# Weight splits moved into the norms, roots by a GpSimd power, and three smaller moves in a two-block transformer kernel

## The chip, the cores and the metric

One core of one Trainium2 chip. The metric is the device time of one execution in microseconds (us); the median of several executions is compared. Weights and activations are in fp32, in DRAM at the start; the output goes back to DRAM. Five engines take part, each with its own queue of instructions that it runs in order: TensorE (PE: matmul; PEld: its weight loads), VectorE (DVE), ScalarE (ACT), GpSimd (POOL) and SyncE (SP, which only issues DMAs here).

## The reference

256 tokens of width 1024 go through two blocks. The first mixes (block attention beside a gated linear recurrence, hgrn2), then has a product-key expert layer (PEER). The second has two layers with adaptive modulation: an even one (convolution beside an RG-LRU) and an odd one (stick-breaking attention), each with a SwiGLU feed-forward.

```python
def rmsnorm(x, g):
    y = x * lax.rsqrt(jnp.mean(x * x, axis=-1, keepdims=True) + 1e-6)
    return y * g

# first block
xn = rmsnorm(h, norm1_g)
q_a, k_a, v_a, q_r, f_r, i_r, g_r = split(xn @ w_in)
h = h + concat([moba_attention(q_a, k_a, v_a), hgrn2(q_r, f_r, i_r, g_r, lb, rec_norm_g)]) @ w_out
h = h + peer(rmsnorm(h, norm2_g), wq, subkeys, peer_u, peer_v)
x = rmsnorm(h, normf_g)

# hgrn2: f = lb + (1-lb)*sigmoid(f_pre), per head and chunk
scores = einsum('bhtd,bhtsd,bhsd->bhts', qc, exp(min(cum_t - cum_s, 0)), kc)   # decay products
o = rmsnorm(o, norm_g) * silu(g)

# peer: top 16 of 128 x 128 keys per head
gates = softmax(sc)                       # sc: the 16 best scores
out = einsum(gates * gelu(xb @ u[eidx]), v[eidx])

# second block, each layer
sh_m, sc_m, g_m, sh_f, sc_f, g_f = split(silu(c) @ ada_w + ada_b)
x = x + g_m * mixer(rms_norm(x, mix_norm) * (1 + sc_m) + sh_m)
hf = rms_norm(x, ffn_norm) * (1 + sc_f) + sh_f
x = x + g_f * ((silu(hf @ w_gate) * (hf @ w_up)) @ w_down)
# odd mixer: q = rms_norm(qkv[0], q_norm), k = rms_norm(qkv[1], k_norm), per head of 64
```

## The kernel before

All products are in fp32 precision, made of three matmuls of split operands: every weight half (128x1024, 512 KB, one DMA on SP into `raw`, L180) is split into `hi`, a cast on ScalarE (L197), and `lo = raw - hi`, on VectorE (L198), on GpSimd for six units of wq and six of pu. Two halves are a unit. The weights form one stream in a fixed order: wp (input projection), wo, wq (queries), pu and pv (experts), wi0, wo0, fgu0, fd0, wi1, wo1, fgu1, fd1. `unit` (L203) hands out a unit and loads the next one; at the last three units of wo, pv and fd it loads two ahead, so that two units of the next stream are there when that stream's norm runs. There are four `raw` buffers, and three (in places eight) of `hi` and `lo`.

In front of wp, wq, wi0, fgu0, wi1 and fgu1 stands a norm, `norm_t` (L403). For each half of the tokens `t` (128 tokens) it adds the residual (`add_res`: L778, or L781 and L782 with a gate row), squares on ScalarE with a sum (L480), adds the sums up into `m` (L428; L434 to L436 where a second gain row comes in), takes its root with `rsqrt1` (L379: a guess by integer arithmetic and three Newton steps, eight VectorE operations), scales an identity by it (`dr`, L440), turns the tokens on TensorE by 16 matmuls with `dr` (L448), and makes `y` (ScalarE, L451) and its split `xh` and `xl` (L458, L459). After the first half of the tokens, `ahead` (L328) multiplies it with the first two units, whose `hi` and `lo` must be there; the second half is normed beside that and multiplied in `out_n512` (L308), whose result is then copied out by ScalarE (L345), and the following unit's splits are queued behind that copy (`evict`, L226).

In mix1 the recurrence makes the decay products chunk by chunk: differences (L609, L611), their exponentials (ScalarE, L612), then the product with the keys on GpSimd (L613) and with the queries on VectorE (L614); L641 does the cross part. At the end each half of the tokens goes through a root of 128x4 (`rsqrt`, L365: ten VectorE operations), the gate product `o` (L759, L760), transposes, and the copy `ch` (L765), the operand of wo. Attention logits are `lg` (L661).

In peer the routing runs as a generator, one step per expert, beside the expert matmuls. `gains` (L869) is the softmax of the gates: a difference `gr` on VectorE (L872), two steps, an Exp for each token half on ScalarE (L876), a step, and the normalising (L880 to L882). ScalarE's other work there is the experts' activation `actA` (L990), of another function table, so that each change of function costs a table load (ACT_TABLE_LOAD). In the odd layer `qk` (L1316) takes roots of 128x8 (L1326) for queries and keys.

The adaptive modulation (`ada_steps`, L1081) is a second background: 96 products of 128x1024 on VectorE (L1118), each with its own 512 KB DMA `araw`, taken one step at a time by the loops of the other stages, in the even layer by `chunk` (L1215).

The order of work on each engine is made by a list scheduler, which takes the program's order as priority; `issue_after(ins)` says that what follows is queued behind `ins` on that engine. `self.after` holds the last two operations of a norm, behind which later splits are queued.

Of the kernel before, what the change touches and what calls it, by code (L numbers as in the profile page):

```python
# [137 lines left out]
class Prog:  # L138
# [4 lines left out]
    def stream_init(self):  # L143
# [10 lines left out]
        self.pending = []  # L154
        self.nload = 0
# [18 lines left out]
    def load(self, n, hs=(0, 1)):  # L174
        nc = self.nc
        nm, j = self.order[n]
        halves = self.ready.setdefault(n, [])
        for h in hs:
            s = self.wp.tile([128, 1024], F32, name="raw", bufs=self.RAWB)
            self.last_load = nc.sync.dma_start(s, self.i[nm][j][:, h * 1024:(h + 1) * 1024])  # L180
            pool, bufs = self.wp, self.SPB
            if self.roomy(n):
                if self.ring % (self.SPB + self.EXT) >= self.SPB:
                    pool, bufs = self.ext, self.EXT
                self.ring += 1
            else:
                self.ring = 0
            hi = pool.tile([128, 1024], F32R, name="hi", bufs=bufs)
            lo = pool.tile([128, 1024], F32R, name="lo", bufs=bufs)
            a, b = self.POOLED.get(nm, (0, 0))  # L190
            eng = nc.gpsimd if a <= j < b else nc.vector
            with ExitStack() as es:
                for i in self.after:
                    es.enter_context(self.tc.issue_after(i))
                if self.evicted is not None:
                    es.enter_context(self.tc.issue_after(self.evicted.ins))
                nc.scalar.copy(hi, s)  # L197
                ins = eng.tensor_tensor(lo, s, hi.bitcast(F32), op=ALU.subtract)  # L198
            if eng is nc.vector:
                self.last_lo = ins  # L200
            halves.append((hi, lo))

    def unit(self, nm, j):  # L203
# [8 lines left out]
        if self.nload <= upto:  # L212
            self.load(self.nload, (0,))
            self.half = self.fresh = True
        return self.ready.pop(n)

    half = fresh = False

    def rest(self):

        if self.half:
            self.half = False
            self.load(self.nload, (1,))
            self.nload += 1
# [136 lines left out]
    def guess(self, y, x):  # L361

        self.nc.vector.tensor_scalar(y.bitcast(I32), x.bitcast(I32), -0.5, float(0x5f3759df), op0=ALU.mult, op1=ALU.add)

    def rsqrt(self, pool, v, n, scale):  # L365

        nc = self.nc
        x = pool.tile([128, n], F32, name="rx", bufs=2)
        y = pool.tile([128, n], F32, name="ry", bufs=2)
        z = pool.tile([128, n], F32, name="rz", bufs=2)  # L370
        nc.vector.tensor_scalar(x, v, scale, EPS, op0=ALU.mult, op1=ALU.add)
        self.guess(y, x)
        for _ in range(3):
            nc.vector.tensor_tensor(z, y, y, op=ALU.mult)
            nc.vector.scalar_tensor_tensor(z, z, -0.5, x, op0=ALU.mult, op1=ALU.mult)
            nc.vector.scalar_tensor_tensor(y, z, 1.5, y, op0=ALU.add, op1=ALU.mult)
        return y

    def rsqrt1(self, pool, x):  # L379

        nc = self.nc
        m = pool.tile([128, 1], F32, name="rm", bufs=4)
        y = pool.tile([128, 1], F32, name="r1", bufs=4)
        z = pool.tile([128, 1], F32, name="r2", bufs=4)
        self.guess(y, x)
# [794 lines left out]
    def even(self):  # L1180
# [34 lines left out]
        def chunk(n):  # L1215
# [3 lines left out]
            if n % 2:  # L1219
                next(st, None)  # L1220
# [227 lines left out]
```

## Time and profile before

| what | us |
|---|---|
| median of 3 runs | 1647.27 (1646.49 to 1650.29) |
| the profiled execution | 1649.3 |
| its span in the profile | 1647.5 |
| TensorE busy | 1591.6 |
| VectorE busy | 1253.1 |
| ScalarE busy | 868.9 |
| GpSimd busy | 80.3 |

The mean granted TensorE clock over the span was 0.992 of full speed. Three views were read: the page's first part for the share of each engine; the list of what TensorE waited for, one line for each pair of waiting and releasing line; and the timeline around the waits, in which a figure in brackets after an instruction is the engine's idle time before it, with what ended it. A stretch's granted clock comes from the table of stretches; 1.00 is the upper level (2.4 GHz), 0.50 the lower (1.2 GHz), and a value between is a mean over both.

### The profile page before, as it was taken

What the parts mean: (1) busy time and instruction counts of PE and PEld (TensorE: products, weight loads), DVE (VectorE), ACT (ScalarE), POOL (GpSimd) and SP (SyncE); (2) the same over time, 40 slices, a digit from 0 to 9 for tenths busy, and PEclk for the clock granted to TensorE, in tenths of its full rate; (3) what the DMA queues carried; (4) which work ended last, traced back from release to release, by engine and by line L of the source; (5) the groups of instructions that cost most, each with busy time, mean ns of one, the idle gap of its engine ahead of it and who ended that gap; (6) DMA issues with size and microseconds to landing.
All of it is one profiled execution on the core that took longest, in us unless ns stands there. A gap on an engine that the chain in (4) does not pass through costs nothing.

```text
span 1647.5 us, 25992 instructions
## 1 busy us (share of the span) xinstructions
PE 1591.6 (97%) x9406; PEld 1394.1 (85%) x9406; DVE 1253.1 (76%) x2840; ACT 868.9 (53%) x1581; POOL 80.3 (5%) x47
## 2 busy tenths in 40 slices
PE   7999998999999999999999998999999999999998
PEld 6877898999999999888887886887888877778887
DVE  5987489958888898777778777886888778656553
ACT  5654554545444444455555555745444477755441
POOL 0120481000000000000000000000000000000000
PEclk9999999999999999999999999999999999999999
DMA  6435354644444444877778876565999653327552
GB/s 205 141 104 168 104 179 143 207 139 151 146 152 150 146 151 152 283 264 262 271 272 271 270 270 206 179 229 186 336 333 333 244 195 119 102 94 242 185 186 72
DMA packets 89041, 323.00 MB, mean 196 GB/s; under 512 B 9904, under 2 KB 10320, under 8 KB 88784
## 3 DMA queue, kind: packets, MB, share of 16 engines
q1 hardware_dynamic: 87904, 317.88, 56.7%
q10 hardware_dynamic: 1008, 3.47, 0.6%
q8 instruction: 73, 1.20, 0.3%
q14 instruction: 56, 0.46, 0.1%
HBM read 320.24 MB, written 1.06 MB: 195 GB/s over the span
## 4 chain that ended last, share of the span: by engine, by line
PE 82%; DVE 8%; ACT 5%; DMA 4%; issue 2%; ACTq 0%; DVEq 0%; SPq 0%
PE acc L277 16%; PE acc L279 16%; PE acc L278 16%; PE pt L249 8%; PE pt L250 8%; PE pt L253 8%; PE acc L976 3%; DVE lo L198 2%; ACT hi L197 2%; DMA raw<-in_wi 1%; PE pt L448 1%; DMA raw<-in_wo 1%; ACT y L451 1%; PE pt L620 1%; ACT jk L480 1%
## 5 line engine op out<-in xcount | busy, mean ns | idle before, releaser
L198 DVE TENSOR_TENSOR lo<-raw,hi 128x1024 fp32r<-128x1024 f32 x476 | 580.7, 1224 | 245.3 <-ACT hi L197 236.9
L197 ACT CAST hi<-raw 128x1024 fp32r<-128x1024 f32 x500 | 523.3, 1051 | 385.5 <-PE acc L279 144.3
L249 PE MATMUL pt<-xh,hi 128*128 128x256 f32 x1344 | 336.9, 288 | 11.7 <-ACT actA L990 6.8
L250 PE MATMUL pt<-xl,hi 128*128 128x256 f32 x1344 | 330.8, 284 | 0.0
L249 PEld LDWEIGHTS pt<-xh,hi 128*128 128x128 f32 x1344 | 258.0, 192 | 13.7 <-ACT actA L990 7.5
L250 PEld LDWEIGHTS pt<-xl,hi 128*128 128x128 f32 x1344 | 258.4, 192 | 0.4 <-issue 0.3
L277 PE MATMUL acc<-hi,xh 128*128 128x512 f32 x544 | 217.5, 400 | 6.6 <-ACT xh L458 6.6
L279 PE MATMUL acc<-hi,xl 128*128 128x512 f32 x544 | 213.4, 392 | 0.6 <-DVE xl L459 0.6
L278 PE MATMUL acc<-lo,xh 128*128 128x512 f32 x544 | 213.0, 391 | 0.0
L279 PE MATMUL acc<-hi,wl 128*128 128x512 f32 x512 | 199.3, 390 | 2.2 <-DVE wl L358 2.2
L277 PE MATMUL acc<-hi,wh 128*128 128x512 f32 x512 | 199.6, 390 | 1.6 <-ACT wh L357 1.6
L278 PE MATMUL acc<-lo,wh 128*128 128x512 f32 x512 | 199.2, 389 | 0.5 <-DVE lo L198 0.5
L253 PE MATMUL pt<-xh,lo 128*128 128x256 f32 x1344 | 192.0, 285 | 0.4 <-DVE lo L198 0.4
L253 PEld LDWEIGHTS pt<-xh,lo 128*128 128x128 f32 x1344 | 173.9, 192 | 1.4 <-issue 0.7
L277 PEld LDWEIGHTS acc<-hi,xh 128*128 128x128 f32 x544 | 102.3, 188 | 30.2 <-ACT xh L458 8.9
L279 PEld LDWEIGHTS acc<-hi,xl 128*128 128x128 f32 x544 | 102.4, 188 | 24.8 <-DVE xl L459 3.5
L278 PEld LDWEIGHTS acc<-lo,xh 128*128 128x128 f32 x544 | 102.7, 189 | 20.1 <-DVE lo L198 0.3
L1118 DVE SCALAR_TENSOR_TENSOR araw<-araw,sc 128x1024 f32<-128x1024 f32 x96 | 116.8, 1218 | 0.0
L279 PEld LDWEIGHTS acc<-hi,wl 128*128 128x128 f32 x512 | 96.0, 188 | 24.2 <-DVE wl L358 4.3
L277 PEld LDWEIGHTS acc<-hi,wh 128*128 128x128 f32 x512 | 96.1, 188 | 22.5 <-ACT wh L357 2.8
L278 PEld LDWEIGHTS acc<-lo,wh 128*128 128x128 f32 x512 | 96.1, 188 | 20.7 <-DVE lo L198 0.9
L974 DVE TENSOR_SCALAR B<-iota,idxT,idxT 128x128 f32<-128x128 f32 x256 | 87.1, 340 | 0.0
(303 smaller groups left out, 1981.4 us busy)
## 6 DMA issues: line engine op xcount, KB each, us to landing
raw<-in_pu SPq DMA_DIRECT2D x128, 512.0 KB, 3.9
raw<-in_pv SPq DMA_DIRECT2D x128, 512.0 KB, 5.2
araw<-in_ada SPq DMA_DIRECT2D x96, 512.0 KB, 5.5
raw<-in_fgu SPq DMA_DIRECT2D x88, 512.0 KB, 5.5
raw<-in_wi SPq DMA_DIRECT2D x44, 512.0 KB, 5.0
raw<-in_fd SPq DMA_DIRECT2D x44, 512.0 KB, 4.5
raw<-in_wp SPq DMA_DIRECT2D x28, 512.0 KB, 4.8
raw<-in_wo SPq DMA_DIRECT2D x24, 512.0 KB, 4.4
```

The costliest lines, as they stand in the source:

```text
L197: nc.scalar.copy(hi, s)
L198: ins = eng.tensor_tensor(lo, s, hi.bitcast(F32), op=ALU.subtract)
L249: nc.tensor.matmul(out, hi[:, c], xh[:, k, ts], start=k == 0, stop=False)
L250: ins = nc.tensor.matmul(out, hi[:, c], xl[:, k, ts], start=False, stop=False)
L253: nc.tensor.matmul(out, lo[:, k * 128:k * 128 + 128], xh[:, k, ts], start=False, stop=k == K - 1)
L277: nc.tensor.matmul(a, xh, hi[:, cs], start=first, stop=False)
L278: nc.tensor.matmul(a, xh, lo[:, cs], start=False, stop=False)
L279: ins = nc.tensor.matmul(a, xl, hi[:, cs], start=False, stop=last)
L448: nc.tensor.matmul(pt[:, k], src[:, o:o + 128], dr, start=True, stop=True)
L974: nc.vector.tensor_scalar(B, iota, idxT[1][:, t:t + 1], idxT[2][:, t:t + 1], op0=ALU.is_equal, op1=ALU.mult)
L976: nc.tensor.matmul(gp[:, n], A, B, start=True, stop=True)
L1118: nc.vector.scalar_tensor_tensor(w, w, 1.0, self.sc, op0=ALU.mult, op1=ALU.mult, accum_out=m[:, k:k + 1])
```

## The change

1. `load` is parted into the DMA and `split_raw`, the cast and the subtraction. At the last unit of wo, pv and fd (`put_off`) the second unit of the next stream is loaded, but its two splits are put off; for wp it is the first unit's. They are made in `norm_t` at the first half of the tokens: the first queued behind the last square and `m`, the second behind that square and `dr`.
2. `rsqrt1` and `rsqrt` become `root`: one GpSimd tensor_tensor with `pow` and -0.5 (14 calls of 128x1, 2 of 128x4, 8 of 128x8). `rsqrt` keeps its scaling (one VectorE operation).
3. The decay products (L613, L641) and the gate's product with `rng` (L741) go from GpSimd to VectorE, ten instructions.
4. In `gains` one Exp of both token halves, eight steps after the difference in place of two.
5. `out_n512` after a norm loads the third unit ahead of the matmuls of the second half of the tokens.
6. The copy `ch` is made an `evict`, so that later splits of wo are queued behind it.
7. `chunk` takes no ada step at its last two odd numbers (17 and 19); they are taken by later loops.

```diff
-    def load(self, n, hs=(0, 1)):
+    def load(self, n, hs=(0, 1), late=False):
+        for h in hs:
...
+            self.last_load = self.nc.sync.dma_start(s, self.i[nm][j][:, h * 1024:(h + 1) * 1024])
+            self.raws.append((n, s))
+            if not late:
+                behind = list(self.after)
+                if self.evicted is not None:
+                    behind.append(self.evicted.ins)
+                self.split_raw(behind)
+
+    def split_raw(self, behind):
...
+        with ExitStack() as es:
+            for i in behind:
+                es.enter_context(self.tc.issue_after(i))
+            nc.scalar.copy(hi, s)
+            ins = eng.tensor_tensor(lo, s, hi.bitcast(F32), op=ALU.subtract)
...
         if self.nload <= upto:
-            self.load(self.nload, (0,))
+            self.put_off = upto == n + 2 and self.order[n + 1][0] != nm
+            self.load(self.nload, (0,), self.put_off)
...
+    def next_unit(self, n):
+        if self.nload == n:
+            self.load(n)
+            self.nload += 1
...
     def out_n512(self, nm, j0, x, first=None, step=None):
         us, acc = first or ([], [[self.acc([128, 512])], None])
+        if first:
+            self.next_unit(self.pos[(nm, j0)] + 2)
...
+    def root(self, pool, x, n=1):
+        y = pool.tile([128, n], F32, name="ry", bufs=4)
+        self.nc.gpsimd.tensor_tensor(y, x, self.mhalf if n == 1 else self.mhalf.to_broadcast([128, n]), op=ALU.pow)
+        return y
...
-                r = self.rsqrt1(tp, m)
+                r = self.root(tp, m)
+                if t == 0:
+                    self.split_raw([sq_ins, m_ins.ins])
                 dr = tp.tile([128, 128], F32, name="dr", bufs=2)
                 dr_ins = nc.vector.tensor_scalar(dr, self.ident, r, None, op0=ALU.mult).ins
+                if t == 0:
+                    self.split_raw([sq_ins, dr_ins])
...
-        self.load(0)
+        self.load(0, late=True)
...
-            nc.gpsimd.tensor_tensor(xv[:, :, 0], xv[:, :, 0], kv[:, :, 0], op=ALU.mult)
+            nc.vector.tensor_tensor(xv[:, :, 0], xv[:, :, 0], kv[:, :, 0], op=ALU.mult)
...
-            nc.gpsimd.tensor_tensor(gs[:, t], gs[:, t], rng, op=ALU.mult)
+            nc.vector.tensor_tensor(gs[:, t], gs[:, t], rng, op=ALU.mult)
...
-            nc.scalar.copy(ch[:, 4:8, ts], pt)
+            self.evict(nc.scalar.copy(ch[:, 4:8, ts], pt))
...
-                yield
-                yield
-                for t in range(2):
-                    nc.scalar.activation(gr[t], gr[t], AF.Exp)
+                for _ in range(8):
+                    yield
+                nc.scalar.activation(gr2, gr2, AF.Exp)
...
-            if n % 2:
+            if n % 2 and n < 16:
                 next(st, None)
```

## Rows read from the trace of the kernel before

**Rows 1.** Busy time, share of the span and instructions of each engine (page, part 1).

```profile
PE 1591.6 (97%) x9406; PEld 1394.1 (85%) x9406; DVE 1253.1 (76%) x2840; ACT 868.9 (53%) x1581; POOL 80.3 (5%) x47
```

**Rows 2.** What TensorE waited for: us in total, times, longest; engine and line waited for.

```profile
PE pt L448 <- DVE dr L440: 13.9, 5, 8.3
PE pt L249 <- ACT actA L990: 6.8, 2, 6.4
PE pt L249 <- ACT hi L197: 4.9, 3, 1.6
PE pt L620 <- DVE lg L661: 3.2, 2, 2.4
```

**Rows 3.** Timeline, start, duration, [idle before, releaser]: the gates' Exp and the expert after it.

```profile
268.00 0.31 ACT L876 ACTIVATE gr<-gr 128x128 f32<-128x128 f32 x1 [6.93 <-DVE gr L872]
270.06 0.58 PE L249 MATMUL pt<-xh,hi 128*128 128x256 f32 x1 [6.43 <-ACT actA L990]
280.08 2.35 DVE L198 TENSOR_TENSOR lo<-raw,hi 128x1024 fp32r<-128x1024 f32 x2
288.26 1.12 PE L253 MATMUL pt<-xh,lo 128*128 128x256 f32 x8
```

**Rows 4.** Stretches: length, busy time (instructions) of PE, PEld, DVE, ACT, POOL, granted clock, DMA.

```profile
265.00:270.00 5.00, 0.00 (x0) 0.00 (x0) 5.00 (x33) 1.97 (x3) 0.00 (x0) 0.73 0.01 2
270.00:275.00 5.00, 4.94 (x26) 4.94 (x27) 5.00 (x15) 4.94 (x8) 0.00 (x0) 0.59 0.68 207
155.00:160.00 5.00, 5.00 (x19) 3.80 (x18) 4.33 (x6) 2.60 (x3) 0.00 (x0) 0.69 0.74 231
```

**Rows 5.** Timeline around the third unit of wp.

```profile
29.16 0.58 ACT L345 COPY xx<-acc 128x512 f32<-128x512 f32 x1 [1.53 <-PE acc L279]
30.75 0.39 PE L249 MATMUL pt<-xh,hi 128*128 128x256 f32 x1 [1.62 <-ACT hi L197]
```

**Rows 6.** Timeline of the norm in front of fgu0.

```profile
1112.76 1.22 DVE L198 TENSOR_TENSOR lo<-raw,hi 128x1024 fp32r<-128x1024 f32 x1 [0.85 <-ACT hi L197]
1113.90 0.68 DVE L782 TENSOR_TENSOR h<-h,gy 128x512 f32<-128x512 f32 x1
1118.68 0.16 DVE L428 SCALAR_TENSOR_TENSOR m<-m,m 128x1 f32<-128x1 f32 x1 [0.79 <-ACT jk L480]
1120.47 0.29 DVE L440 TENSOR_SCALAR dr<-ident,r 128x128 f32<-128x128 f32 x1
1120.81 3.58 PE L448 MATMUL pt<-dr,h 128*128 128x128 f32 x16 [3.09 <-DVE dr L440]
```

**Rows 7.** Timeline of the norms in front of wi0 (second half) and fgu1.

```profile
1030.27 2.05 PE L448 MATMUL pt<-dr,hf 128*128 128x128 f32 x16 [1.71 <-DVE dr L440]
1451.32 3.37 PE L448 MATMUL pt<-dr,h 128*128 128x128 f32 x16 [2.56 <-issue]
```

**Rows 8.** Lines L613 and L614 (duration ns min/median/max), and the smallest fill on POOL.

```profile
L613 POOL TENSOR_TENSOR xx<-xx,kk x7: 1282/2042/2921, 55.1 to 102.2; 128x512 f32<-128x512 f32 x7
L614 DVE TENSOR_TENSOR xx<-xx,q x7: 678/693/1984, 55.6 to 103.2; 128x512 f32<-128x512 f32 x7
L1439 POOL MEMSET const-float32-1.0<- 128x1 f32 x1 | 0.1, 98 | 0.0
```

**Rows 9.** The eight-wide root's steps of one line, grouped: busy us, mean ns | idle before.

```profile
L376 DVE SCALAR_TENSOR_TENSOR ry<-rz,ry 128x8 f32<-128x8 f32 x24 | 3.9, 163 | 0.2
```

**Rows 10.** Timeline of the end of mix1.

```profile
149.56 0.69 DVE L760 TENSOR_TENSOR o<-o,ry 128x512 f32<-128x512 f32 x1
150.09 1.05 ACT L197 CAST hi<-raw 128x1024 fp32r<-128x1024 f32 x1 [1.70 <-DMA raw<-in_wo]
153.99 0.50 PE L277 MATMUL acc<-hi,ch 128*128 128x512 f32 x1 [2.39 <-ACT ch L765]
```

**Rows 11.** Timeline ahead of the out projection wo0.

```profile
1091.29 1.22 DVE L1118 SCALAR_TENSOR_TENSOR araw<-araw,sc 128x1024 f32<-128x1024 f32 x1
1094.04 0.50 PE L278 MATMUL acc<-lo,yh 128*128 128x512 f32 x1 [1.16 <-DVE lo L198]
```

More of the change, by code (lines that the diff above doesn't have):

```diff
@@ L154, in stream_init @@
         self.pending = []
+        self.raws = []
         self.nload = 0
@@ L175, in load @@
+    def split_raw(self, behind):
+        if not self.raws:
+            return
         nc = self.nc
+        n, s = self.raws.pop(0)
         nm, j = self.order[n]
[L177 to L201, printed above, removed]
@@ new lines, in split_raw @@
+        pool, bufs = self.wp, self.SPB
+        if self.roomy(n):
+            if self.ring % (self.SPB + self.EXT) >= self.SPB:
+                pool, bufs = self.ext, self.EXT
+            self.ring += 1
+        else:
+            self.ring = 0
+        hi = pool.tile([128, 1024], F32R, name="hi", bufs=bufs)
+        lo = pool.tile([128, 1024], F32R, name="lo", bufs=bufs)
+        a, b = self.POOLED.get(nm, (0, 0))
+        eng = nc.gpsimd if a <= j < b else nc.vector
+        with ExitStack() as es:
[3 more added lines that the diff above has]
+            ins = eng.tensor_tensor(lo, s, hi.bitcast(F32), op=ALU.subtract)
@@ L203, in unit @@
+        if eng is nc.vector:
+            self.last_lo = ins
+        self.ready.setdefault(n, []).append((hi, lo))
     def unit(self, nm, j):
@@ L222, in rest @@
             self.half = False
-            self.load(self.nload, (1,))
+            self.load(self.nload, (1,), self.put_off)
             self.nload += 1
@@ L358, in split @@
         self.nc.vector.tensor_tensor(lo, src, hi.bitcast(F32), op=ALU.subtract)
-    def guess(self, y, x):
-        self.nc.vector.tensor_scalar(y.bitcast(I32), x.bitcast(I32), -0.5, float(0x5f3759df), op0=ALU.mult, op1=ALU.add)
+    def root(self, pool, x, n=1):
+        y = pool.tile([128, n], F32, name="ry", bufs=4)
+        self.nc.gpsimd.tensor_tensor(y, x, self.mhalf if n == 1 else self.mhalf.to_broadcast([128, n]), op=ALU.pow)
+        return y
     def rsqrt(self, pool, v, n, scale):
-        nc = self.nc
         x = pool.tile([128, n], F32, name="rx", bufs=2)
[L369 to L385, printed above, removed]
-        nc.vector.tensor_scalar(m, x, -0.5, None, op0=ALU.mult)
-        for _ in range(3):
-            nc.vector.scalar_tensor_tensor(z, y, m, y, op0=ALU.mult, op1=ALU.mult)
-            nc.vector.scalar_tensor_tensor(y, z, 1.5, y, op0=ALU.add, op1=ALU.mult)
-        return y
-    def mean2(self, pool, h, jk):
-        nc = self.nc
-        H = D // 2
-        a = pool.tile([128, 1], F32, name="m2a", bufs=4)
-        b = pool.tile([128, 1], F32, name="m2b", bufs=4)
-        nc.scalar.activation(jk[:, 0:H], h[:, 0:H], AF.Square, scale=D ** -0.5, accum_out=a)
-        nc.vector.scalar_tensor_tensor(jk[:, H:D], h[:, H:D], 1.0 / D, h[:, H:D], op0=ALU.mult, op1=ALU.mult,
-                                       accum_out=b)
-        return a, b
+        self.nc.vector.tensor_scalar(x, v, scale, EPS, op0=ALU.mult, op1=ALU.add)
+        return self.root(pool, x, n)
     def norm_t(self, pool, side, nm, gain, shift=None, row=None, more=None):
@@ L466, in norm_t @@
                 for t in range(2):
-                    r1 = self.rsqrt1(tp, m1s[t])
+                    r1 = self.root(tp, m1s[t])
                     nc.vector.tensor_scalar(h[t], srcs[t], r1, None, op0=ALU.mult)
@@ L865, in sums @@
                         yield
-            gr = [p2.tile([128, 8, 16], F32, name=f"gr{t}") for t in range(2)]
+            gr2 = p2.tile([128, 2, 8, 16], F32, name="gr2")
+            gr = [gr2[:, t] for t in range(2)]
             def gains():
```

21 lines of the change are left out of this document (13 added, 8 removed).

## The prediction

> **What bounds the kernel now.** I read the page first: TensorE is busy 97% of the span, VectorE 76%, GpSimd 5% [rows 1]. So the kernel is at its end when TensorE has run its 9406 matmuls, none of which the change removes, and an edit can pay only where TensorE stands still or runs at the lower of its two clock levels because it stood still just before. The list of TensorE's waits [rows 2] is therefore the budget: the reader should see that it is short, and that each line names one part of this change. `dr` holds 13.9 us of it (8.3 of that is the start of the program), the gate path's `actA` 6.8, `hi` 4.9, the logits of mix1 3.2. Then I looked at each wait in the timeline, to see what was queued ahead of the instruction that came last.
>
> **Part by part.**
>
> *Exponentials of the gates (a).* ScalarE's Exp waited 6.93 us for `gr`, and could start at 268.00, in a stretch in which VectorE was busy without a gap [rows 3, 4]; ScalarE runs in order, so expert activations (`actA`) sat behind it, and TensorE waited 6.43 us and went on at 270.06. Six steps later, `gr` is long there and the wait is gone. The pause is paid twice: in the 5 us after it the granted clock was 0.59 [rows 4], so 5 x (1 - 0.59) = 2.05 us more go to the same work. Together 8.5 us at most. What is late next is VectorE, which is behind with `lo`: the pair of `lo`s at 280.08 takes 2.35 us, so its first is there at 281.3, and its expert's last matmuls start at 288.26 [rows 3]; pulled in by 8.5 us they would want it at 279.8, 1.5 us too early. The three normalising operations that move later with the Exp give some of that back. I take 7.5 us, between 5 (the next `lo`s late too) and 8.5.
>
> *Third unit's fetch (c).* Three times (wp, wq, wi0) TensorE waits 1.62 us for a `hi` whose cast stands on ScalarE behind the eviction of the block just finished (the copy at 29.16, the matmul at 30.75) [rows 5]; the three are the 4.9 us of [rows 2]. The change puts the cast ahead of the second token half's matmuls, when ScalarE is idle. It frees all three: 4.9 us, 0 at worst if the data were not there.
>
> *Split inside the norm, in front of fgu0 (d).* Here the second unit's splits stand in front of the residual adds: a `lo` of 1.22 us goes at 1112.76, VectorE having waited 0.85 us for its `hi`, and the add that makes `h` follows only at 1113.90; each token half is made of two such columns, and the second has such a `lo` ahead of it too. Then `m` at 1118.68, `dr` at 1120.47, and TensorE waits 3.09 us [rows 6]. With both splits behind the square and `dr`, the adds follow the accumulators directly and I place `dr` over 2 us earlier, and the root takes another 1 us off: the wait goes. The clock comes back too: the 16 transposes took 3.58 us here, 2.05 in the norm of wi0 [rows 6, 7], so 1.5 are lost to the clock. Gain 4.6, between 2 and 4.6. The four split halves now fall between `dr` and the first `y` or `xl`, and that is a new wait, costed below.
>
> *Roots (B).* From `m` to `dr` is 1.79 us now [rows 6]: `m` 0.16 and eight small operations. One GpSimd operation takes their place. No row shows this power. Nearest from below is a GpSimd fill of 128x1, 0.10 us, and from above a GpSimd product of 128x512 alone, 1.28 us [rows 8]. I take 0.4 us, since 128x1 is nearest the fill, and 0.2 for the two handoffs between engines; so 1.79 - 0.16 - 0.6 = 1.0 us less where the root is exposed, from 0.2 to 1.3 by the bounds. Exposed is the second token half in front of wi0, where TensorE waits 1.71 us for `dr` [rows 7]: gain (e) 1.0, from 0 to 1.7. In front of fgu1 the 2.56 us put down to "issue" [rows 7] ends at the same operation `dr`, but there the first put-off split may be queued ahead of `dr`, so 0.2 (f), from -1 to 1. Of the 13.9 us that TensorE waits for `dr` in five places [rows 2], the start's 8.3, the 3.09 of fgu0 and this 1.71 leave 0.8 for all others, so in front of wq and wi1 a faster root brings nothing; at the start, where tokens and weights are still arriving, I take 0 too, from 0 to 1. The eight roots of 128x8 in odd's qk are ten operations each, of 0.16 us and their gaps [rows 9], so about 2 us; a power over eight elements may take longer than one over one: 0 (g), from -3 to 1.
>
> *End of mix1 (b).* Two four-wide roots are interleaved one small step at a time with `lo`s of 1.22 us, so the product `o` that needs the first root starts only at 149.56, and TensorE waits 2.39 us for `ch` [rows 10]; in the next 5 us the granted clock is 0.69 [rows 4], 1.55 us. As one operation the root is done before the first of these `lo`s. What comes up in its place is the weights: a `hi` of wo waits 1.70 us for its DMA until 150.09 [rows 10], and now the other splits of wo stand behind the copy of `ch`. I take 2.5 of the 3.9, from 0.
>
> *Products of decay on VectorE (h).* GpSimd takes 1.28 to 2.92 us for one, VectorE for the partner product of the same shape 0.68 to 1.98, with a median of 0.69 [rows 8]. Ten come over: 10 x 0.69 = 6.9 us more on VectorE, the busier engine; what the two engines cost each other when both run (up to 2.92 - 1.28 = 1.6 and 1.98 - 0.68 = 1.3 us an instance) goes. What I count on is that the chain of each step shortens by 1.28 - 0.69 = 0.6 us or more and that part of the 3.2 us for `lg` [rows 2], behind it on VectorE, goes. I take 1.5, from -1 to 3. The Trainium skill (GPSIMD Engine Reference, 1 Specifications) has it that GpSimd shares its SBUF interfaces with VectorE, with contention for instructions with two SBUF inputs; the rows agree (0.68 against 1.98). Its 4.1 Engine selection gives two-input elementwise work to VectorE as about twice as fast, which the rows bear out here too (1.28 against 0.68) and which speaks against the roots' move (rival 3).
>
> *Ada steps (i).* Of the wait for `lo` at 1094.04, 1.16 us, the cause is an ada product of 1.22 us at 1091.29 just ahead of it on VectorE [rows 11]. Two such steps go to the down projection later. Their fetches go with them on SP's queue, to a stretch where the same kind of step already runs. I take 1.1, from 0 to 1.2.
>
> *The sum.* 7.5 + 2.5 + 4.9 + 4.6 + 1.0 + 0.2 + 0 + 1.5 + 1.1 = 23.3 us. Against it stand new waits: in norms with TensorE standing, `hi`s (1.05 us each) and `lo`s (1.22) in front of the first `y` and `xl`, which I put at 0.5 us in four norms, and 1.2 for wo's splits behind `ch`: 3.2. Left is 20.1 us. The profiled run took 1649.3 us with its span of 1647.5, and 2 us lie between it and the median 1647.27: 1649.3 - 20.1 = 1629.2 for a run like the profiled one, and 1647.27 - 20.1 = 1627.2, **1627**, for the median.
>
> **Rivals.**
>
> 1. *The split blocks the norm.* If a `lo` is queued ahead of `dr` and waits for its `hi`, each exposed norm (wi0, fgu0, fgu1, wp) pays 1.05 + 1.22 = 2.3 us, less the 0.5 already in the sum: 4 x 1.8 = 7 us, and 1634. For it: `split_raw` is called ahead of `dr` in the program. Against it: the `hi` must come first, and the power will mostly be through before it.
>
> 2. *VectorE's backlog replaces the wait of the gates.* VectorE is busy without a gap from 265 to 275 [rows 4]; if its `lo`s come no earlier than now, of 8.5 us only about 3 are left: 4.5 us less, about 1632. For it: the `lo` is short by 1.5 us at the very first. Against: the load that moves with the Exp is small.
>
> 3. *Slower: the power is dear.* If one takes p us, each exposed root loses p - 0.4 against my sum. Exposed are five in norms, one in mix1, and some four of odd's eight: ten. The change then turns at 20.1 = 10 x (p - 0.4), that is at p = 2.4 us; at 1.28 us, the row of a GpSimd product alone, the time would be 1627.2 + 10 x 0.88 = 1636, and at 4 us 1627.2 + 10 x 3.6 = 1663. For it: no row has a power, and GpSimd's products need 1.28 to 2.92 [rows 8]. Against: those have 512 elements in a partition, not one to eight. The Trainium skill (GPSIMD Engine Reference, 2.1 Instruction dispatch) gives about 6 us, once, for the first call of a freshly loaded kernel; no row here shows one, and once on wp's path it would by estimate make 1633.
>
> 4. *The edits do not do it.* The order of instructions is made anew by priority, and if the same waits return under other names (`hi` behind `ch`, decay products in a full VectorE), 1640 to 1648.
>
> **How the numbers follow.** Forecast 0.50 (1622 to 1631); better, with no new waits and (a) whole, 0.10 (1614 to 1622); rival 1 0.15; rival 2 0.10; rival 3 0.09 (of it 0.06 slower, the rest between 1630 and 1644); rival 4 0.06 (in it 0.05 of no change, 0.01 slower). For the range I leave out rival 3's upper part and half of rival 4: 1615 to 1641. A measurement can tell about 0.2%, or 3.3 us, from no change: faster 0.88, same 0.05, slower 0.07.
>
> **What would show it.** Right: no TensorE pause near 264 to 270 and a granted clock of 1.00 after it; no 1.62 us waits on `hi`; in front of fgu0 `gy` directly follows the accumulators and `dr` comes before TensorE ends; a power under 1 us between `m` and `dr`. Wrong: a wait of TensorE on `dr` with a `lo` just ahead of it (rival 1); waits on `lo` from 270 to 300 (rival 2); powers over 2 us, or `qn` in the list of waits above 1 us a time (rival 3); the sum of TensorE's waits within 4 us of now (rival 4). What would make the prediction wrong in its size is the clock: if it falls elsewhere after a shorter pause, some 3.5 us of the gain go.

## The result and the profile after

The changed kernel takes 1627.51 us (median of 4 runs, 1626.15 to 1628.63), the kernel before 1648.12 in the same comparison: a ratio of 0.9874, 95% interval 0.9857 to 0.9891. The forecast was 1627, with a range of 1615 to 1641. The total is right; its parts are not, and that is what the rest is about.

The page's first part and the list of TensorE's waits (us in total, times, longest) of the changed kernel, which answer to [rows 1, 2]:

```profile
PE 1581.8 (97%) x9406; PEld 1388.5 (85%) x9406; DVE 1225.7 (75%) x2639; ACT 866.2 (53%) x1578; POOL 85.9 (5%) x61
...
PE pt L445 <- DVE dr L435: 10.8, 1, 10.8
PE pt L269 <- ACT actA L989: 7.1, 1, 7.1
PE acc L297 <- ACT xh L455: 5.9, 10, 0.7
PE acc L299 <- DVE xl L456: 3.2, 6, 1.2
```

L445 is the transpose of the norms (L448 before), L269 the first expert matmul (L249), L989 the experts' activation (L990). `dr` is waited for once, at the start, where it was five times; the waits for `hi` in front of L249 and for `lg` are gone; the wait for `actA` is still there.

Both kernels run the same 9406 matmuls in nearly the same order, so the start of the k-th matmul in one trace against the other says how much had been saved by then. By stage (profiled runs: 1649.3 and 1626.15 us, spans 1647.5 and 1624.3):

| stage, in the trace of before (us) | forecast | measured |
|---|---|---|
| first block of wp, norm included (0 to 28) | 0 - 0.5 | 1.7 |
| third unit of wp, wq, wi0 (c) | 4.9 | 1.9 + 2.1 + 2.1 = 6.1 |
| recurrence of mix1 (33 to 117) (h) | 1.5 | 4.2 |
| end of mix1 and norm of wq (117 to 173) (b) | 2.5 - 1.2 | 2.0 |
| experts with routing (188 to 305) (a) | 7.5 | -0.4 |
| end of the experts, norm of wi0 (to 1034) (e) | 1.0 - 0.5 | 2.3 |
| even mixer to wo0 (1042 to 1099) (i) | 1.1 | 1.9 |
| end of wo0, norm of fgu0 (1099 to 1131) (d) | 4.6 - 0.5 | 5.2 |
| fgu0, fd0, odd mixer (1131 to 1436) (g) | 0 | -3.2 |
| norm of fgu1 (1436 to 1465) (f) | 0.2 - 0.5 | 3.3 |
| together | 20.1 | 23.1 |

The medians are 20.6 us apart; the profiled runs lie one at the upper and one at the lower side of their medians. The largest term missed by 8 us, and all the others together were 11 us better: that the sum came out on 1627 is luck.

**The root.** The groups on GpSimd (count, busy us, mean ns, idle before with its releasers) and the product beside the decay on VectorE (minimum, median, maximum in ns):

```profile
L386 POOL TENSOR_TENSOR ry<-rx,n 128x8 f32<-128x8 f32 x8 | 13.0, 1638 | 61.9 <-DVE rx L392 61.9
L386 POOL TENSOR_TENSOR ry<-m,n 128x1 f32<-128x1 f32 x14 | 7.9, 569 | 1137.4 <-PE acc L299 763.3 <-DVE m L421 364.8 <-DVE m L429 9.4
L386 POOL TENSOR_TENSOR ry<-rx,n 128x4 f32<-128x4 f32 x2 | 2.1, 1028 | 102.9 <-DVE rx L392 102.9
...
L613 DVE TENSOR_TENSOR xx<-xx,q x7: 682/684/686, 52.6 to 101.2; 128x512 f32<-128x512 f32 x7
```

A power takes 0.57 us for one element in a partition, 1.03 for four, 1.64 for eight: I had 0.4 for one. With GpSimd out of the way the partner product of the decay takes 0.68 us each time, where it went up to 1.98 [rows 8].

**In front of fgu0**, answering to [rows 6]:

```profile
1092.61 0.68 DVE L780 TENSOR_TENSOR gy<-acc,g 128x512 f32<-128x512 f32 x1
...
1096.38 0.54 POOL L386 TENSOR_TENSOR ry<-m,n 128x1 f32<-128x1 f32 x1 [74.30 <-DVE m L421]
...
1096.95 0.29 DVE L435 TENSOR_SCALAR dr<-ident,ry 128x128 f32<-128x128 f32 x1 [0.66 <-POOL ry L386]
...
1098.45 1.72 PE L445 MATMUL pt<-dr,h 128*128 128x128 f32 x14
```

`dr` is done 1.2 us before TensorE comes to the transposes, which carry no wait now and run 0.11 us apart. From the start of `m` (1096.14) to that of `dr` it is 0.81 us, where it was 1.79.

**In front of wp** my first rival happened:

```profile
6.30 0.54 POOL L386 TENSOR_TENSOR ry<-m,n 128x1 f32<-128x1 f32 x1 [5.86 <-DVE m L421]
8.21 1.04 ACT L209 CAST hi<-raw 128x1024 fp32r<-128x1024 f32 x1 [2.17 <-DMA raw<-in_wp]
9.28 1.22 DVE L210 TENSOR_TENSOR lo<-raw,hi 128x1024 fp32r<-128x1024 f32 x1 [3.06 <-ACT hi L209]
10.43 0.28 DVE L435 TENSOR_SCALAR dr<-ident,ry 128x128 f32<-128x128 f32 x1
```

The root is there at 6.84, but `lo` stands ahead of `dr` on VectorE and waits for a `hi` that waits for its weights: `dr` comes 2.5 us later than before. That loss is gone by 22 us: from 15 us on TensorE waits for nothing. From 15 to 25 us, of the changed kernel and then of the kernel before (length, busy us of PE, PEld, DVE, ACT, POOL, granted clock, DMA):

```profile
15.00:25.00 10.00, 10.00 (x53) 8.46 (x52) 5.61 (x14) 8.07 (x21) 0.50 (x2) 1.00 0.35 125
```

```profile
15.00:25.00 10.00, 8.31 (x35) 6.58 (x36) 4.36 (x15) 4.72 (x17) 0.00 (x0) 0.83 0.38 133
```

TensorE, late but with all its operands there, has no gap and the full clock; before, it stood 1.7 us and ran at 0.83.

**In front of the gates** the same wait stands, answering to [rows 3]:

```profile
256.31 0.42 ACT L875 ACTIVATE gr<-gr 128x256 f32<-128x256 f32 x1 [7.58 <-DVE gr L872]
258.47 0.58 PE L269 MATMUL pt<-xh,hi 128*128 128x256 f32 x1 [7.05 <-ACT actA L989]
```

Counted on ScalarE, Exp stands behind the eighth `actA` in both kernels. In the program it comes six steps later, in the queue at the same place.

### The profile page after: what moved, and what is told of

Read it like the earlier page. It is cut to its first block, busy times and chain, and to the rows that moved or that the text cites. A ratio compares the mean times of both kernels' runs of the same rounds, so it can differ in the third digit from the quotient of the medians.

```text
span 1624.3 us, 25807 instructions
## 1 busy us (share of the span) xinstructions
PE 1581.8 (97%) x9406; PEld 1388.5 (85%) x9406; DVE 1225.7 (75%) x2639; ACT 866.2 (53%) x1578; POOL 85.9 (5%) x61
## 4 chain that ended last, share of the span: by engine, by line
PE 82%; DVE 8%; DMA 5%; ACT 3%; issue 1%; POOL 0%; SPq 0%; ACTq 0%; DVEq 0%; POOLq 0%
PE acc L299 16%; PE acc L297 16%; PE acc L298 16%; PE pt L269 8%; PE pt L270 8%; PE pt L273 8%; PE acc L975 4%; DVE lo L210 2%; DMA raw<-in_fgu 2%; ACT hi L209 1%; PE pt L619 1%; DMA raw<-in_wo 1%; PE pt L445 1%; DMA raw<-in_wi 1%; PE pt L1347 1%
## 5 line engine op out<-in xcount | busy, mean ns | idle before, releaser
L269 PE MATMUL pt<-xh,hi 128*128 128x256 f32 x1344 | 336.6, 288 | 7.1 <-ACT actA L989 7.1
L269 PEld LDWEIGHTS pt<-xh,hi 128*128 128x128 f32 x1344 | 258.2, 192 | 8.1 <-ACT actA L989 7.5
```

Of the source, the lines that this page charges most:

```text
L269: nc.tensor.matmul(out, hi[:, c], xh[:, k, ts], start=k == 0, stop=False)
```

## The experiments

Each is the changed kernel with one edit, unless said otherwise. The runs were made in three groups on chips where the kernel before took 1643.4, 1645.2 and 1646.9 us; times of two groups are compared by their ratio to it (the changed kernel: 0.9874), and stages by the start of the same matmul, against the trace of the changed kernel or of the first run below, which is nearly the same kernel on the first of these chips. Most stages that an edit does not touch repeat within some 0.6 us between such traces, the start and the first decay steps within 2. Three places come and go by 0.7 to 1.7 us whatever the edit: the end of the experts (600 to 1000 us), a wait for `fy` near 1231 us, and a fall of the clock near 1305 us (run 10).

**1. Exp as before.**

```diff
-                for _ in range(8):
+                for _ in range(2):
                     yield
-                nc.scalar.activation(gr2, gr2, AF.Exp)
+                for t in range(2):
+                    nc.scalar.activation(gr[t], gr[t], AF.Exp)
```

> The changed kernel with one part undone: the gates' Exp two steps after the difference and one for each half of the tokens, as before. Theory: the eight steps changed nothing, because in both kernels Exp stands on ScalarE behind the same eighth actA and waits for the same gr (6.93 us before, 7.58 after); so the time stays within 1.5 us of 1627.5, Exp stands behind the eighth actA again, and TensorE's wait for actA is 6 to 7.5 us. The second Exp with its two table loads costs ScalarE 3 us of idle time and TensorE nothing. Rival: the eight steps did help and something else took the gain; then this is slower by 4 us or more, and the wait for actA is over 10 us.

1625.65 us, ratio 0.9889 (0.9871 to 0.9908), a span of 1624.0 against 1624.3. Exp stands behind the eighth `actA`, and TensorE waits 6.8 us in two places for it. Place and wait are as the theory had them, and from 230 to 310 us the trace keeps within 0.2 us of the changed kernel's: this part of the change moves nothing. The time cannot tell: it is 1.9 us under 1627.5, but on another chip, and by the ratio some 2.5 us over, with intervals that overlap.

**2. Exp queued behind a late `actA`.**

```diff
+                with self.tc.issue_after(self.acted.ins):
-                nc.scalar.activation(gr2, gr2, AF.Exp)
+                    nc.scalar.activation(gr2, gr2, AF.Exp)
...
-                    nc.scalar.activation(cells(i2, slice(0, 256)), pt, AF.Gelu)
+                    self.acted = nc.scalar.activation(cells(i2, slice(0, 256)), pt, AF.Gelu)
```

> The changed kernel, with Exp queued behind the last actA that stands ahead of it in the program (some 14 experts later on ScalarE's queue than now). Theory: Exp no longer waits, the 7.05 us that TensorE waits for actA go, and with them about 2 us x 0.35 x 2 of low clock in the 10 us after it; 1627.5 - 8 = 1619 to 1620, if VectorE's lo keeps up. Rival (the prediction's second): VectorE, busy without a gap through 265 us, becomes late with lo; then TensorE waits for lo instead, 3 to 6 us in all between 255 and 290, and the time is 1623 to 1626.

1628.22 us, ratio 0.9907 (0.989 to 0.9923): no gain. Exp now stands behind 22 `actA`. Against run 1, 8.0 us are saved at the matmul that starts at 256.8, 3.8 at 264, 1.7 at 290 and 0.3 at 304. The timeline where the first part goes, and the stretch from 230 to 310 us:

```profile
262.53 1.04 ACT L209 CAST hi<-raw 128x1024 fp32r<-128x1024 f32 x1 [6.16 <-DMA raw<-in_pu]
263.48 0.38 ACT L990 ACTIVATE actA<-pt 128x256 f32<-128x256 f32 x1
263.91 0.39 PE L269 MATMUL pt<-xh,hi 128*128 128x256 f32 x1 [4.24 <-ACT actA L990]
...
230.00:310.00 80.00, 73.25 (x590) 72.24 (x589) 79.80 (x215) 34.64 (x51) 12.88 (x6) 0.98 0.46 156
```

VectorE is busy 79.8 of 80 us. The wait still bears the name `actA`, but what stands ahead of it on ScalarE is a `hi` that waited 6.16 us for its weights. The fetch needs a free `raw`, and a `raw` comes free with its `lo`, which VectorE has not come to. What the DMA queue waited for from 225 to 320 us (in all, times, longest) is mostly that; the two other lines are from the timeline where Exp now stands:

```profile
SPq L180 <- DVE lo L210: 44.5, 17, 8.9
...
300.25 1.28 ACT L990 ACT_TABLE_LOAD   x1
...
301.98 0.39 PE L269 MATMUL pt<-xh,hi 128*128 128x256 f32 x1 [1.22 <-ACT actA L990]
```

This is the prediction's second rival, and more than I had put it (of 8.5 us about 3 left): by 290 us the backlog, with the low clock behind its wait, has taken 6.3 of the 8.0. Of the rest Exp itself takes 1.5, because in its new place TensorE waits behind its change of function table.

**3. Six units of pu without `lo`** (the subtraction is left out and `hi` multiplied in its place).

```diff
+        skip = nm == "pu" and 6 <= j < 12
-        lo = pool.tile([128, 1024], F32R, name="lo", bufs=bufs)
+        lo = hi if skip else pool.tile([128, 1024], F32R, name="lo", bufs=bufs)
...
+            if not skip:
-            ins = eng.tensor_tensor(lo, s, hi.bitcast(F32), op=ALU.subtract)
+                ins = eng.tensor_tensor(lo, s, hi.bitcast(F32), op=ALU.subtract)
```

> The changed kernel with the subtraction left out for six units of pu (the seventh to the twelfth): their hi is multiplied in place of lo, so that part of the expert products is left out, with as many matmuls as before. It takes twelve lo of 1.22 us, 14.6 us, off VectorE between 235 and 290 us and puts nothing on GpSimd. Theory: it is VectorE's queue that the gates wait for; gr then comes 8 us or more earlier and the 7.05 us wait for actA goes, with the low clock behind it: 1617 to 1620 on a chip where the changed kernel takes 1626. With the run of twelve units on GpSimd this tells what GpSimd's share cost: there the same lo left VectorE and 14.3 us were lost. Rival: Exp's place in ScalarE's queue is what counts, and the wait stays above 4 us.

1627.0 us, ratio 0.9885 (0.9862 to 0.9907). The theory as I had put it falls, the rival holds by its sign, a wait above 4 us:

```profile
253.18 0.42 ACT L877 ACTIVATE gr<-gr 128x256 f32<-128x256 f32 x1 [4.32 <-DVE gr L874]
...
255.34 0.58 PE L271 MATMUL pt<-xh,hi 128*128 128x256 f32 x1 [7.22 <-ACT actA L991]
```

`gr` is there 3 us earlier, and Exp has gone up to behind the seventh `actA`: the order of the queue is made anew for a VectorE with less to do, and again too early. After it, nothing more is waited for up to 330 us, as in the changed kernel. The theory could not have come out here: from 225 us to `gr` the changed kernel has only two `lo` on VectorE (at 246.0 and 247.9), and this run none, so 2.4 us of `lo` were all that stood ahead of `gr`. The rest of VectorE's unbroken work up to `gr` is the routing itself. So there are two causes, one behind the other: Exp's place, ahead of activations while `gr` is still being made (runs 1 and 3), and, once Exp is out of the way, VectorE's backlog of `lo` (run 2). Both edits together were not tried, so that the 7 us can be had is argued only.

**4. Twelve units' `lo` on GpSimd, and 5. the same with Exp behind a late `actA`.**

```diff
-    POOLED = {"wq": (2, 8), "pu": (0, 6)}
+    POOLED = {"wq": (2, 8), "pu": (0, 12)}
```

> The changed kernel with the lo of twelve of pu's units on GpSimd rather than six: twelve more lo of 2.41 us there, twelve of 1.22 us (14.6 us in all) fewer on VectorE up to about 270 us. Exp as in the changed kernel, behind the eighth actA. Theory: VectorE, busy without a gap from 220 to 310 us, is what the gates' stretch waits for; with 14.6 us less in its queue gr is there some 8 us earlier, most of the 7.05 us wait for actA goes and does not come back: 1617 to 1621 on a chip where the changed kernel takes 1626. Rival: GpSimd's long products slow VectorE's two-input operations beside them (0.68 to 1.98 us in the decay products) by as much as they take off; then 1624 to 1628. Second rival: Exp's place alone is the cause; then gr comes earlier but something else still stands in front, and less than 3 us are gained.

> The same twelve units on GpSimd, and Exp queued behind a later actA as in the run with Exp pinned. Theory: pinned alone, the wait moved from actA at 258 to the same actA at 264 and later, by way of lo, raw and hi, so pinning pays only where VectorE has time left. Here it has: no wait over 1 us for actA between 240 and 310 us, and the time 0 to 2 us under that of the run with twelve units alone. Rival: VectorE is still late, the waits are 3 us or more, and the time is no better than the changed kernel's.

1641.15 us, ratio 0.9972 (0.9957 to 0.9987), and 1636.76, ratio 0.9949 (0.9934 to 0.9965): run 4 is worse than any of its rivals had it, and in run 5 the rival holds, and by far. The wait for `actA` is 18.3 and 17.9 us. From the timeline of run 4:

```profile
248.27 4.82 POOL L210 TENSOR_TENSOR lo<-raw,hi 128x1024 fp32r<-128x1024 f32 x2
248.39 5.25 DVE L855 TENSOR_TENSOR cand<-v 128x128 f32<-128x128 f32 x4
...
264.78 2.48 DVE L905 SCALAR_TENSOR_TENSOR ab<-ab,ab 128x128 f32<-128x128 f32 x1
269.57 3.42 DVE L914 TENSOR_TENSOR oh<-iota,ab 128x1024 f32<-128x1024 f32 x1
```

The same operations in the changed kernel, where GpSimd has no `lo` after 241.5 us:

```profile
247.09 0.89 DVE L855 TENSOR_TENSOR cand<-v 128x128 f32<-128x128 f32 x4
...
262.67 0.28 DVE L905 SCALAR_TENSOR_TENSOR ab<-ab,ab 128x128 f32<-128x128 f32 x1
264.20 1.22 DVE L914 TENSOR_TENSOR oh<-iota,ab 128x1024 f32<-128x1024 f32 x1
```

VectorE's products beside GpSimd's are stretched by 2.2 us each, a small one as much as a large one. The four `cand` lose 4.4 us together; they stand in the routing ahead of `gr`, for which Exp waits 10.3 us. Run 3 takes the same `lo` away and gives GpSimd nothing: 1641 against 1627. That difference is the price of the `lo` on GpSimd; the runs do not part what VectorE loses beside them from what they take themselves, 2.4 us each for 1.22. The Trainium skill (GPSIMD Engine Reference, 1 Specifications) says that GpSimd shares its SBUF interfaces with VectorE, with contention for VectorE's instructions with two SBUF inputs; these numbers agree.

**6. Products of decay back on GpSimd.**

```diff
-            nc.vector.tensor_tensor(xv[:, :, 0], xv[:, :, 0], kv[:, :, 0], op=ALU.mult)
+            nc.gpsimd.tensor_tensor(xv[:, :, 0], xv[:, :, 0], kv[:, :, 0], op=ALU.mult)
```

(and the cross part and gate by `rng` likewise)

> The changed kernel with the ten products (decay, and gate by rng) back on GpSimd. Theory: the 4.2 us that the changed kernel gains from 60 to 113 us come from these products, by the shorter chain (0.68 us for 1.28 to 2.92) and by VectorE's partner operations that are no longer stretched to 1.98 us; so TensorE's two waits for lg, 3 us, come back with the low clock behind one of them, and the time is 3 to 5 us above the changed kernel's. Rival: the gain there is that of a different order of instructions; then the stretch is as fast as in the changed kernel.

1628.48 us, ratio 0.9909 (0.9873 to 0.9946). In the stretch the theory holds: against run 1 it loses 4.8 us between 58 and 114 us, and the wait is back under its old name:

```profile
PE pt L619 <- DVE lg L660: 3.2, 2, 2.5
```

Against the trace of the changed kernel it loses 4.4. At its end it is only 1.3 and 0.9 us behind these two, because places that the edit does not touch went better in it: the whole time tells less than the stretch.

**7. No early third unit.**

```diff
-        if first:
-            self.next_unit(self.pos[(nm, j0)] + 2)
```

> The changed kernel without the early fetch of the third unit. Theory: the three waits for hi of 1.62 us come back in front of the third unit of wp, wq and wi0, and with the weight loads' own delay some 2 us each: 5 to 6 us above the changed kernel's time. Rival: with the norms changed, ScalarE has time for these casts anyway, and less than 2 us come back.

1635.74 us, ratio 0.9938 (0.9923 to 0.9954). The list of waits has them again, three of 1.6 us:

```profile
PE pt L269 <- ACT hi L209: 4.9, 3, 1.6
```

In the order of matmuls the three places lose 1.9, 2.1 and 1.9 us against run 1, 5.9 in all, as expected. The whole loses more: 1.5 us go near 1305 us with the clock (run 10), and 3.6 between 1330 and 1345 us in the odd mixer, where TensorE waits 2.2 us for a transposed `qk`; why the order there changed with this edit I did not find out.

**8. Roots of 128x1 by Newton steps.** `rsqrt1` as before, called in both places of `norm_t`.

```diff
-                r = self.root(tp, m)
+                r = self.rsqrt1(tp, m)
```

> The changed kernel with the fourteen roots of 128x1 by Newton steps on VectorE as before; those of 128x4 and 128x8 stay on GpSimd. Theory: m to dr is 0.91 us with the power (0.55 us for itself) and 1.79 with the steps, so 0.9 us come back in the norm of wi0 (second half) and of fgu1, about 0.9 in front of fgu0 if TensorE now waits there, and in front of wp nothing, because lo stands between m and dr: 1.5 to 3 us above the changed kernel's time. Rival: the eight steps also stand among the put-off lo on VectorE and get interleaved with them as at the end of mix1; then 5 us or more.

1631.62 us, ratio 0.9904 (0.9883 to 0.9926), its span 6.0 us longer than the changed kernel's. That is nearer to the rival's 5 us than to the theory, but 1.6 of the 6.0 lie in the first decay steps, where run 1 has them too. At the start TensorE is 2.5 us earlier (8.2 us), and that is gone by 26 us. In the norms of wi0 and fgu0 it waits four times for `dr`, 2.1 us in all, and loses 1.4 and 0.7; in front of fgu1 2.2 us are lost in one place, where a step stands behind a `lo` as in the rival:

```profile
1434.51 2.98 PE L474 MATMUL pt<-dr,h 128*128 128x128 f32 x16 [1.84 <-DVE dr L464]
```

**9. Splits of the second unit ahead of the norm again** (wp excepted).

```diff
-            self.put_off = upto == n + 2 and self.order[n + 1][0] != nm
+            self.put_off = False
```

> The changed kernel with no split put off except that of wp: the second unit's two splits are queued before the norm's own work again, at wq, wi0, fgu0, wi1 and fgu1. Theory: in front of fgu0 the adds stand behind the lo again and dr comes after TensorE has run out: 2 to 3 us of wait there and 1.5 of low clock; elsewhere nothing, except that in front of wi1 and fgu1 the loss of 1.4 us for late xl gets smaller. In all 2.5 to 4.5 us above the changed kernel's time. Rival: the roots alone make up for it, and it is within 1.5 us.

1632.75 us, ratio 0.9921 (0.9899 to 0.9942), span 5.2 us longer. In front of fgu0 3.4 us are lost, and the `lo` stands ahead of `gy` again:

```profile
1097.39 1.22 DVE L210 TENSOR_TENSOR lo<-raw,hi 128x1024 fp32r<-128x1024 f32 x1 [0.85 <-ACT hi L209]
1098.53 0.68 DVE L780 TENSOR_TENSOR gy<-acc,g 128x512 f32<-128x512 f32 x1
...
1103.21 3.45 PE L445 MATMUL pt<-dr,h 128*128 128x128 f32 x16 [3.07 <-DVE dr L435]
```

In front of fgu1 TensorE stands 1.6 us with no releaser listed, which I had not expected, and 0.8 us of it are left after the norm. So there each of the two, root (run 8) and split, undone alone, takes back a part of the changed kernel's gain of 3.3. The rest of the 5.2 lies in the first decay steps, as in run 8, and near 1305 us (run 10).

**10. Both put-off splits behind `dr`.**

```diff
-                if t == 0:
-                    self.split_raw([sq_ins, m_ins.ins])
...
                 if t == 0:
                     self.split_raw([sq_ins, dr_ins])
+                    self.split_raw([sq_ins, dr_ins])
```

> The changed kernel with both put-off splits queued behind the square and dr. Theory: in the norm of wp the first lo stands ahead of dr on VectorE and waits for a hi whose weights land only at 8.2 us; dr then comes at about 7.1 us in place of 10.4 and TensorE starts its transposes 3.3 us earlier, at 7.4. But what follows waits for the same weights and for the second half of the tokens, so of the 3.3 us at most 1.5 are left by the time the second unit is multiplied: 1626 to 1627.5. In the norms of fgu0 and fgu1 dr was first already: nothing changes there. Rival: the start is worth its full 2.5 us: 1625 or less.

1626.5 us, ratio 0.9893 (0.9874 to 0.9911). `dr` at 6.91 us, and TensorE starts 2.9 us earlier than in run 1:

```profile
7.25 3.78 PE L444 MATMUL pt<-dr,h 128*128 128x128 f32 x16 [7.25 <-DVE dr L433]
...
12.96 0.63 PE L298 MATMUL acc<-lo,xh 128*128 128x512 f32 x1
```

0.9 to 1.9 us of it are left at 16 to 27 us, 0.2 at 154: the theory, but for one thing. From 12.96 to 15 us the matmuls take 0.63 us where 0.40 is usual, while the record has the granted clock at 1.00. Around the norm of wi1 1.5 us are lost, which is not this edit's doing, and in all it is 0.9 us slower than run 1 on the same chip. The stretch there, of this run and then of the changed kernel:

```profile
1304.00:1312.00 8.00, 6.77 (x23) 4.67 (x23) 6.29 (x9) 6.13 (x12) 0.22 (x1) 0.79 0.14 40
```

```profile
1304.00:1312.00 8.00, 6.79 (x29) 5.18 (x30) 7.01 (x10) 6.51 (x12) 0.09 (x1) 1.00 0.27 78
```

The same waits of 0.65 and 1.23 us are followed by a granted clock of 0.79 here and of 1.00 there. Runs 4, 9 and 12 show the 0.79 too, run 7 a like fall; runs 1 to 3, 5 and 6 do not.

**11. Roots of 128x8 by Newton steps.**

```diff
-        return self.root(pool, x, n)
+        return self.newton(pool, x, n) if n == 8 else self.root(pool, x, n)
```

> The changed kernel with the eight roots of 128x8 in odd's qk by Newton steps on VectorE as before; all other roots stay on GpSimd. Theory: the product qn that waits for the power (1.64 us for one) blocks VectorE, which runs in order, so xl came 1.23 us late for TensorE and more was lost in the same stretch; the 2.8 us that the changed kernel loses from the norm of wi1 to the end of the attention come back by half or more: 1624.5 to 1626. The wait of TensorE for xl of 1.2 us goes. Rival: the loss there has other causes (the order of the splits in the norm of wi1); then 1627 to 1628, and the stretch takes as long as now.

1627.58 us, ratio 0.9892 (0.9868 to 0.9916): no gain. The wait of the changed kernel

```profile
1302.45 1.65 POOL L386 TENSOR_TENSOR ry<-rx,n 128x8 f32<-128x8 f32 x1 [1.05 <-DVE rx L392]
1304.13 0.69 DVE L1326 TENSOR_TENSOR qn<-acc,ry 128x512 f32<-128x512 f32 x1 [1.76 <-POOL ry L386]
...
1305.20 0.50 PE L299 MATMUL acc<-hi,xl 128*128 128x512 f32 x1 [1.23 <-DVE xl L456]
```

goes, and 1.6 us with it, as the theory had it: VectorE waits for the power, and `xl` stands behind. But some 30 us on 4.2 us are lost, where the steps are interleaved with `lo`, one by one, and 2.7 of them are left at 1376 us:

```profile
1333.10 1.23 DVE L210 TENSOR_TENSOR lo<-raw,hi 128x1024 fp32r<-128x1024 f32 x1
1334.25 0.16 DVE L402 SCALAR_TENSOR_TENSOR ny<-nz,ny 128x8 f32<-128x8 f32 x1
...
1335.28 0.30 PE L1365 MATMUL pt<-ident,qn 128*128 128x128 f32 x1 [1.59 <-DVE nz L401]
```

So in this kernel the power of 128x8 costs a wait at one place and saves more at others.

**12. The copy of `ch` not marked.**

```diff
-            self.evict(nc.scalar.copy(ch[:, 4:8, ts], pt))
+            nc.scalar.copy(ch[:, 4:8, ts], pt)
```

> The changed kernel with the copy of ch no longer marked, so that wo's splits are queued as before. Theory: the wait of 1.15 us for the first hi of wo, which now stands behind both copies of ch, goes; if that hi then stands ahead of the second copy, TensorE waits for ch instead. So the end of mix1 gets faster by 0 to 1.2 us: within 1.5 us of the changed kernel. Rival: without the mark several hi stand ahead of ch and the 2.39 us wait of before comes back: 2 us or more above.

1627.52 us, ratio 0.9876 (0.9851 to 0.9901). Against the changed kernel 3.0 us are gained from 137 to 150 us, where no wait of TensorE is left, and 1.6 lost in the norm of wq, in which `xh` is waited for 2.0 us. The mark is worth nothing here: over the two stages it costs 1.4 us (1.1 against run 1). Its price was in my sum at 1.2, and in the changed kernel it shows as one wait of 1.15 us for `hi` behind `ch`:

```profile
138.40 0.59 ACT L764 CAST ch<-pt 128x512 fp32r<-128x512 f32 x1 [1.01 <-PE pt L762]
138.89 2.94 ACT L209 CAST hi<-raw 128x1024 fp32r<-128x1024 f32 x3
...
139.99 1.20 PE L297 MATMUL acc<-hi,ch 128*128 128x512 f32 x4 [1.15 <-ACT hi L209]
```

## Why the prediction was right in sum and wrong in its largest term

*(a), 7.5 us forecast, -0.4 measured.* The step that failed is "six steps later, `gr` is long there and the wait is gone". I took a later place in the program for a later place in ScalarE's queue. Exp stood behind the eighth `actA` in both kernels (run 1): ScalarE was half idle there, and I take it that the scheduler put Exp in where it supposed `gr` to be ready; no run shows its own times. So the sign that I had named, no pause and a clock of 1.00, did not come. Beneath it lies a second error: had Exp moved, VectorE's backlog and Exp's own table loads would have taken nearly the whole gain (run 2). I had seen the `lo` 1.5 us too late and let the three normalising operations count for more than that. Even that 1.5 was misread: counted in the order of the weights, the first `lo` of the pair at 280.08 is multiplied not at 288.26 but one expert earlier:

```profile
285.38 1.12 PE L253 MATMUL pt<-xh,lo 128*128 128x256 f32 x8
```

Pulled in by 8.5 us it would be wanted at 276.9, 4.4 us before it is there. With this row read rightly the term would have been about 4. And a stretch in which VectorE is busy without a gap for 80 us should have been read as its bound.

*(c), 4.9 forecast, 6.1 measured.* Right; undone, the three waits return (run 7). The 1.2 more lie around the waits, not in them.

*(d), 4.1 after its new waits, 5.2 measured.* Right in mechanism and size: splits behind the squares let `gy` follow the accumulators, `dr` is early, and the clock is back. Run 9 shows the splits' share as 3.4, run 8 the root's as 0.7.

*(h), 1.5 forecast, 4.2 measured.* Right in mechanism, the size was off: of the 3.2 us of TensorE's wait for `lg` I counted a half, and left out the low clock behind it. Run 6 takes 4.4 to 4.8 us back.

*(b)* came out at 2.0 for 1.3, with `hi` behind `ch` waiting as I had put it; without the mark it would have been some 1 us more (run 12). *(e)* 2.3 for 0.5 and *(i)* 1.9 for 1.1: I take it that both were held small at waits of TensorE alone. Run 8 brings 1.4 of (e) back; the stage of (e) holds the end of the experts, which also varies without an edit, and (i) and the four-wide roots of (b) were undone in no run.

*(f), -0.3 after its new waits, 3.3 measured.* The term that was mis-sized: I feared that the first put-off `lo` would go ahead of `dr`. It didn't, the root is faster by 0.9, TensorE's own work reaches up to `dr` and the clock does not fall: the 16 transposes take 1.99 us, before 3.37 [rows 7]. Runs 8 and 9 lose 2.2 and 0.8 here.

*(g), 0 forecast, -3.2 measured* from 1131 to 1436, just below the range of -3 to 1 that I gave them. 1.4 of it is the wait for `xl` behind a power of 128x8 (run 11; with the clock behind it, in some traces, 2.9). But the same roots give 1.4 back at 1334 us, where before TensorE waited for `qn` and for a step of its root (0.6 and 0.4 us):

```profile
PE pt L1337 <- DVE qn L1327: 0.6, 1, 0.6
PE pt L1337 <- DVE rz L375: 0.4, 1, 0.4
```

So the eight-wide roots come out at about 0, as forecast, and run 11, which undoes them, does not get the loss back: it is 3.0 us later over this stretch. Another 1.0 is a wait of 1.4 us for `fy` near 1231 us, behind a `lo` and an ada product, where it stood before too. Runs 2, 4 and 6 have no such wait and run 12 has one of 1.5, though none of their edits touches the place, so it is not shown to be the price of (i). For the rest, some 2 us, I have no cause.

*New waits, 3.2.* Of the first rival's four norms only that of wp had `lo` ahead of `dr`, and its 2.5 us were made up within 15 us, as TensorE then neither stood nor ran at a lower clock. The third rival's price never came up: 0.57 to 1.64 us, where it turned at 2.4. The 6 us that the Trainium skill (GPSIMD Engine Reference, 2.1 Instruction dispatch) gives for a first call were not there: the first power starts 0.08 us after `m` and takes 0.54. Whether `pow` is such a freshly loaded kernel no run shows. One sum does not fit its range: no new waits and (a) whole make 1647.27 - 24.3 = 1623, just above the 1614 to 1622 that I gave them.

## What to carry to other kernels

A step moved in a program that a scheduler orders has moved only when its place in the engine's queue has; count what stands ahead of it, and tie it to an instruction if it must wait. An engine that is busy without a gap over a whole stretch should be suspected of being the bound there, whatever name the waits bear; here a wait removed beside it came back under another. A chain of small operations beside long ones on the same engine can pay for the long ones between its links; one operation on an idle engine, though slow, does not, as long as nothing that is waited for is queued behind its reader.

## What the runs showed of the hardware

GpSimd's `pow` as a two-input operation takes 0.57, 1.03 and 1.64 us for 128x1, 128x4 and 128x8: about 0.4 us and 0.15 for each element of a partition. From the end of the operation on VectorE to the start of the power it takes 0.08 us in most places and up to 0.23, from the power to its reader 0.03.

Beside GpSimd's two-input products of 2.4 us, a product on VectorE took 3.42 us for 1.22 (L914) and a small one 2.48 for 0.28 (L905), so both lose about 2.2 us (run 4). Moving 12 `lo` of 1.22 us from VectorE to GpSimd made the kernel 14 us slower than taking them away.

At the start of the program the transposes came 0.22 us apart rather than 0.11, and in run 10 the matmuls after them took 0.63 us rather than 0.40 up to 15 us, with the granted clock recorded as 1.00. In the kernel before matmuls of 0.63 us stand from 18.5 to 20.6 us, where the record has 0.57 (19 to 22 us). So at the start the durations look like the lower level and the record does not; which of them is right the runs do not show.

A wait of 0.65 and one of 1.23 us, 1.3 us apart, were followed by a granted clock of 0.79 over 8 us in the traces of runs 4, 9, 10 and 12 and of 1.00 in those of the changed kernel and of runs 1, 2, 3, 5 and 6, from the same instructions: 1.4 us that come or stay away.
